# The feed-forward's linear half takes its 1/rms behind w_down, and six pairs of w_up instead of five go by seven products

## The chip, the core and the metric

One core of a Trainium2 chip runs the whole program in one launch. The metric is the device time of that launch in microseconds (us). TensorE (PE) does the matrix products; its weight loads are listed apart as PEld. VectorE (DVE) and ScalarE (ACT) do everything between the products, GpSimd (POOL) a little, and SyncE (SP) starts most of the DMA transfers. Sums of products are gathered in PSUM banks of 512 float32 columns; all other data on the core lies in SBUF.

## The reference

The program is a trunk of two layers over 528 tokens (16 learned meta tokens and 512 frames) with 1024 features. Each layer has a mixer, which the change doesn't touch, and a gated feed-forward with a causal convolution over three tokens:

```
n = rms_norm(h, norm_ffn[l])                    # n = h * 1/rms(h, per token) * gain per feature
gate, up = split(n @ w_up, 2)                   # w_up: 1024 x 5632, halves of 2816
gate = causal_dwconv(gate, conv_w)              # 3 taps over tokens, one weight per feature
h = h + (silu(gate) * up) @ w_down              # w_down: 2816 x 1024
```

1/rms is one number per token. The gate half must have it before the convolution and the silu. The linear half, `up`, is only multiplied by something and then summed over features, so a factor per token may stand before or behind w_down. The meta tokens are dropped from the output of the second layer.

## The kernel before, in words

Features lie on the 128 partitions, tokens on the free axis. Every float32 product is made of three passes of TensorE: operands are split into a high part and a rest (`wh` and `wl` of the weights, made by ScalarE at L242 and VectorE at L243; likewise for the activations, by `feed` at L187 and L188), and high x high, high x rest and rest x high are added up in one bank. Below, "product" is one such pass: one matmul instruction of 128 x 128 weights and 264 tokens (or 256, or 512, in the second layer).

w_up runs over 22 pairs j: the gate tile 2j and the linear tile 2j+1, 128 features each. A plain pair is two times 96 products (L268; in the second layer the linear tile takes 48 products of 512 tokens). For each j in the list `UP`, `up7` does both tiles together by Strassen's scheme with seven block products instead of eight, in Winograd's form: two feature tiles by two halves of the tokens, 84 products (L284), with sums of weight blocks (L302 to L305, VectorE) and of result banks (L1097 to L1107, VectorE). Gate banks come from the tags "g" and "a" in turn, the linear half of plain pairs from "s" and "a" in turn, two banks each; `up7` uses g or a, s, and x.

Behind the products of a pair, VectorE multiplies the gate by `rb`, which holds 1/rms of every token on all partitions (L1130, or L1133 while emptying the banks), the convolution and the tanh follow (L1138, L1140, L1141), VectorE multiplies the linear half by `rb` too (L1143 or L1148) and then by the gate `cv` (L1149). The result is split into high part and rest; for the last eight j it is also brought into the sums that the seven products of w_down want.

w_down takes the eight output tiles in four steps of two (m0 = 0, 2, 4, 6). In each step, `strassen` does features 14 to 21 by seven products (84 instructions, L284) and `others` does features 0 to 13 in chunks of four (168 products in layer 0, L1245; products of 512 tokens in most of layer 1). In the first step the seven products come last but one chunk, in the others first. Within the block of seven products, bank X1 is filled, copied by ScalarE into SBUF tile `ts` (L1219), and filled again; X2 is filled; from X1, X2 and the copy VectorE makes four sums in `ts` and `tu` (L1222 to L1227), of 128 x 264 each. They are added to the residual `hk` by `addto` (L1211) before the second chunk of `others` of the step (in the first step before its last chunk). At the end of the step the four banks C are added to `hk` by the same function (or two wide banks at L1263), and in layer 0 each finished `hk` is stored and fed to the next norm: ScalarE makes its high part and its square (L187, L194), VectorE the rest and the sum of squares (L188, L195).

Two things set the order around the change. First, each engine works through its instructions in the order that the compiler's priorities gave, and the splits of weights and the sums of weight blocks have a high priority, so they are put among older work. Second, tiles of one tag share a few buffers: `ts`, `tu`, the tanh `th` and the square `sqt` of `feed` share two (tag "th"); `hk` and `uu` share two; the staged weights have four (`wst`), their split parts three each. An allocation waits until the oldest user of its buffer is done.

Of the kernel before, what the change touches and what calls it, by code (L numbers as in the profile page):

```python
# [11 lines left out]
F32R = mybir.dt.float32r  # L12
# [16 lines left out]
INV = -2e38  # L29
UP = (2, 5, 8, 11, 14)  # L30

# [73 lines left out]
AR = 6720  # L105
# [9 lines left out]
def _trunk(es, tc, nc, a):  # L115
    pool = lambda n, b, **k: es.enter_context(tc.tile_pool(name=n, bufs=b, **k))
    p1 = pool("p1", 1)
# [5 lines left out]
    V, S, G, PE = nc.vector, nc.scalar, nc.gpsimd, nc.tensor  # L123
# [948 lines left out]
    def ffn(l, nf, h1, t0):  # L1072
# [40 lines left out]
        for j in range(FT):  # L1113
            if j == J0:
                far = p1.tile([128, AR], F32R, tag="ar", name="far")
            if j % 2 == 0:
# [10 lines left out]
            if j in UP:  # L1127
                uu = p2.tile([128, T], F32, tag="hk", name="uu", bufs=2)
                up7(j, cs, uu)
                V.tensor_tensor(cs[:, 2 + t0:2 + T], cs[:, 2 + t0:2 + T], rb[:, t0:], op=mul)  # L1130
            else:
                for p, t in ps:
                    V.tensor_tensor(cs[:, 2 + t.start:2 + t.stop], p, rb[:, t], op=mul)  # L1133
# [6 lines left out]
            S.activation(th[:, t0:], cv[:, t0:], AF.Tanh, scale=0.5)  # L1140
            V.scalar_tensor_tensor(cv[:, t0:], th[:, t0:], 1.0, cv[:, t0:], op0=add, op1=mul)  # L1141
            if j in UP:
                V.tensor_tensor(uu[:, t1:], uu[:, t1:], rb[:, t1:], op=mul)  # L1143
            else:
                ps = pu0 if j == 0 else dense(a["w_up"][l, 2 * j + 1], KT, lambda k, part: X[k][:, part], t1, "sa"[j % 2])
                uu = p2.tile([128, T], F32, tag="hk", name="uu", bufs=2)
                for p, t in ps:
                    V.tensor_tensor(uu[:, t], p, rb[:, t], op=mul)  # L1148
            V.tensor_tensor(uu[:, t1:], uu[:, t1:], cv[:, t1:], op=mul)  # L1149
            if j >= J0:  # L1150
# [36 lines left out]
        for m0 in range(0, 8, 2):  # L1187
# [20 lines left out]

            def addto(i, x):
                d = hks[i // 2][:, (s1, s2)[i % 2]]  # L1210
                V.scalar_tensor_tensor(d, x, 0.5, d, op0=mul, op1=add)  # L1211

            def strassen():
                tt = p2.tile([128, T], F32, tag="th", name="ts", bufs=2)
                tu = p2.tile([128, T], F32, tag="th", name="tu", bufs=2)
                P1, U2, U3, U4 = tt[:, :nh], tt[:, nh:2 * nh], tu[:, :nh], tu[:, nh:2 * nh]

# [15 lines left out]
                seven(src, range(J0, FT, 4), S7, sums, X1, X2, C[0], C[1], C[2], first, (one, mid, end))  # L1233
                return P1, U4, U3, U2

# [16 lines left out]
            for k0 in ks[:n]:  # L1252
                others(k0)
            us = strassen()
            for i, k0 in enumerate(ks[n:]):
                if i == 1 or m0 == 0:
                    for c, x in enumerate(us):
                        addto(c, x)
                others(k0)
            for u in range(2):  # L1260
                hk, m = hks[u], m0 + u
                if wide:
                    V.scalar_tensor_tensor(hk[:, t1:], cb[u][:, :2 * nh], 0.5, hk[:, t1:], op0=mul, op1=add)  # L1263
                else:
                    for h in range(2):
                        addto(2 * u + h, C[2 * u + h])
                if last:
                    for t in (s1, s2) if m == 7 else [slice(NM, T)]:
                        nc.sync.dma_start(a["out"][:, m, t.start - NM:t.stop - NM], hk[:, t])
                else:  # L1270
                    t = dr.tile([128, T], F32, name=f"g{l}_{m}")
                    nc.sync.dma_start(t, hk)
                    h2.append(t)
                    nn.feed(m, hk)
# [75 lines left out]
```

## Time and profile before

| | |
|---|---|
| time, median of 3 runs | 1697.04 us (1694.74 to 1697.94) |
| the profiled execution's own time | 1696.78 us |
| its span in the profile | 1695.0 us |
| mean granted clock of TensorE | 0.998 |
| TensorE busy | 1682.9 us, 99% of the span, 13476 instructions |
| VectorE busy | 1360.1 us, 80% |
| ScalarE busy | 819.0 us, 48% |
| GpSimd busy | 75.8 us, 4% |
| DMA | 173.81 MB, mean 103 GB/s |

An engine's busy time is the sum over its instructions, overlaps counted once. The span goes from the first instruction to the last; the execution's own time has what lies around it too. The granted clock is a share of full speed, 1.00 being the level of 2.4 GHz and 0.50 that of 1.2 GHz. In timelines, an instruction's duration goes from its issue to its end; instructions of one engine overlap, so what one costs in a dense stretch is the time from its issue to the next one's issue. An idle time with its releaser is printed in square brackets where the engine stood still.

### The profile page before, as it was taken

The page shows a single profiled execution, that of the slowest core. Times are in us where ns is not written, and L with a number is a line of the kernel's source. Part 1 is how long each engine was busy: PE and PEld are TensorE (multiplying, and loading weights), DVE is VectorE, ACT ScalarE, POOL GpSimd, SP SyncE. Part 2 cuts the span into 40 slices and gives each one's busy share as a digit, 9 for nine tenths or more (in the row PEclk, how much of TensorE's full clock was granted, in tenths as well). Part 3 has the DMA queues.
Part 4 walks back from the last instruction along what each step waited for, and adds up shares of the span by engine and source line. Part 5 has one row for each costly group of instructions (what it writes and reads, how often), then busy time and mean ns, then how long its engine had stood idle before and what let it go on. Part 6 is the DMA issues. An engine that isn't in the chain of part 4 may idle for free.

```text
span 1695.0 us, 35229 instructions
## 1 busy us (share of the span) xinstructions
PE 1682.9 (99%) x13476; PEld 1579.7 (93%) x13476; DVE 1360.1 (80%) x3229; ACT 819.0 (48%) x1779; POOL 75.8 (4%) x190
## 2 busy tenths in 40 slices
PE   9999999999999999999999999999999999999999
PEld 8899988889999999999998999888899999999888
DVE  7899899866788888766558998998767888887754
ACT  6553556553444444434335534566635544444432
POOL 1000111100000000000100000110000000000000
PEclk9999999999999999999999999999999999999999
DMA  6322211225533333234433222112255433333443
GB/s 209 98 64 88 76 46 51 73 75 174 174 121 95 99 94 94 88 104 145 156 103 99 63 88 82 52 45 76 70 176 174 125 94 94 95 98 94 127 123 100
DMA packets 95097, 173.81 MB, mean 103 GB/s; under 512 B 10704, under 2 KB 15536, under 8 KB 94672
## 3 DMA queue, kind: packets, MB, share of 16 engines
q1 hardware_dynamic: 93456, 167.01, 32.5%
q10 hardware_dynamic: 1472, 4.54, 0.7%
q8 instruction: 106, 1.74, 0.4%
q14 instruction: 63, 0.52, 0.1%
HBM read 154.04 MB, written 17.06 MB: 101 GB/s over the span
## 4 chain that ended last, share of the span: by engine, by line
PE 90%; DVE 6%; ACT 3%; issue 1%; DMA 0%; ACTq 0%; DVEq 0%
PE a L268 55%; PE a L284 10%; PE a L1245 9%; PE misc L347 2%; PE iq L347 2%; PE vps L784 2%; PE oBT L947 1%; PE isc L530 1%; PE tps L795 1%; DVE wl L243 1%; PE logit L923 1%; PE PTp L941 1%; PE dS L838 1%; ACT ar L833 0%; ACT wh L242 0%
## 5 line engine op out<-in xcount | busy, mean ns | idle before, releaser
L268 PE MATMUL a<-X,wh 128*128 128x264 f32 (+4 forms) x4208 | 837.1, 295 | 0.6 <-DVE cs L1133 0.6
L268 PEld LDWEIGHTS a<-X,wh 128*128 128x128 f32 x4208 | 666.9, 189 | 17.7 <-issue 1.4
L268 PE MATMUL a<-X,wl 128*128 128x264 f32 (+4 forms) x2104 | 618.4, 294 | 0.0
L242 ACT ACTIVATE wh<-wst 128x512 fp32r<-128x512 f32 (+2 forms) x512 | 309.5, 605 | 537.7 <-PE a L268 284.6
L243 DVE TENSOR_TENSOR wl<-wst,wh 128x512 fp32r<-128x512 f32 (+2 forms) x512 | 335.8, 656 | 153.3 <-ACT wh L242 138.3
L268 PEld LDWEIGHTS a<-X,wl 128*128 128x128 f32 x2104 | 397.9, 189 | 9.1
L1245 PE MATMUL a<-F,wh 128*128 128x264 f32 (+2 forms) x728 | 154.8, 309 | 0.0
L1245 PEld LDWEIGHTS a<-F,wh 128*128 128x128 f32 x728 | 118.0, 188 | 7.3
L1245 PE MATMUL a<-F,wl 128*128 128x264 f32 (+2 forms) x364 | 112.7, 310 | 0.0
L268 PE MATMUL a<-Y,wh 128*128 128x264 f32 (+2 forms) x512 | 92.9, 283 | 0.0
L268 PEld LDWEIGHTS a<-Y,wh 128*128 128x128 f32 x512 | 79.1, 188 | 0.0
L268 PE MATMUL a<-Y,wl 128*128 128x264 f32 (+2 forms) x256 | 72.5, 283 | 0.0
L1245 PEld LDWEIGHTS a<-F,wl 128*128 128x128 f32 x364 | 68.6, 188 | 3.8
L1138 DVE SCALAR_TENSOR_TENSOR cv<-cs,vec,cv 128x528 f32<-128x528 f32 (+1 forms) x88 | 66.7, 758 | 2.7 <-ACT cv L1136 2.1
L405 DVE SCALAR_TENSOR_TENSOR cv<-cs,vec,cv 128x528 f32<-128x528 f32 x72 | 54.4, 758 | 0.9 <-ACT cv L403 0.8
L888 DVE MAX8 m<-ar 128x8 f32<-128x256 f32 (+2 forms) x96 | 53.2, 554 | 1.1
L889 DVE MATCH_REPLACE8 ar<-m,ar 128x256 f32<-128x256 f32 (+2 forms) x96 | 51.9, 541 | 0.0
L268 PEld LDWEIGHTS a<-Y,wl 128*128 128x128 f32 x256 | 48.2, 188 | 0.0
L284 PE MATMUL a<-F,wh 128*128 128x264 f32 (+1 forms) x256 | 47.9, 284 | 0.0
L284 PE MATMUL a<-xar,wh 128*128 128x264 f32 (+1 forms) x240 | 45.6, 283 | 0.0
L1140 ACT ACTIVATE th<-cv 128x528 f32<-128x528 f32 (+1 forms) x44 | 28.1, 638 | 35.7 <-DVE cv L1138 35.6
L284 PE MATMUL a<-X,wh 128*128 128x264 f32 (+1 forms) x240 | 44.8, 283 | 0.0
(401 smaller groups left out, 3057.1 us busy)
## 6 DMA issues: line engine op xcount, KB each, us to landing
wst<-w_up SPq DMA_DIRECT2D x176, 256.0 KB, 2.7
wst<-w_down SPq DMA_DIRECT2D x80, 256.0 KB, 2.7
wst<-w_a SPq DMA_DIRECT2D x64, 256.0 KB, 2.7
wst<-w_gate SPq DMA_DIRECT2D x64, 256.0 KB, 2.9
wst<-w_out SPq DMA_DIRECT2D x32, 256.0 KB, 2.9
hk<-h SPq DMA_DIRECT2D x24, 264.0 KB, 3.5
tg<-gg SPq DMA_DIRECT2D x16, 264.0 KB, 2.2
gr<-tg SPq DMA_DIRECT2D x16, 264.0 KB, 2.7
```

Source lines behind the costliest of these rows:

```text
L242: S.activation(h, w, AF.Copy)
L243: V.tensor_tensor(lo, w, h.bitcast(F32), op=sub)
L268: mms.append(PE.matmul(ps[j][:, :t.stop - t.start], w[:, ws], x[:, t], start=(kk == 0 and w is h and part == 0), stop=(kk == kts - 1 and w ...
L284: PE.matmul(o, ww[:, c:c + 128], x[:, part], start=st, stop=False, skip_group_check=True)
L347: mms.append(PE.matmul(b[:, c:], X[kk][:, part, o:o + 128], w[:, c:], start=(kk == 0 and w is h and part == 0), stop=(kk == KT - 1 and w i ...
L405: V.scalar_tensor_tensor(cv, cs[:, i:i + T], vc(cw + i), cv, op0=mul, op1=add)
L784: PE.matmul(p[r, ch], Ml[r, ch], U[r, ch], start=True, stop=True)
L888: V.max(m8, sc)
L889: V.match_replace(sc, m8, sc, SEL)
L1138: V.scalar_tensor_tensor(cv[:, t0:], cs[:, t0 + i:i + T], vec[:, cw + i:cw + i + 1], cv[:, t0:], op0=mul, op1=add)
L1140: S.activation(th[:, t0:], cv[:, t0:], AF.Tanh, scale=0.5)
L1245: PE.matmul(o, ww[:, 128 * k:128 * k + 128], Yf[k0 + k][:, part, t], start=first(2 * u + h) if k == 0 and part == 0 and ww is w[0] else False,
```

## The change

Two edits. `UP`, the list of pairs of w_up done by seven products, goes from five pairs to six, at other places. And the linear half of the feed-forward is no longer multiplied by 1/rms ahead of the gate: banks (or `uu`) are multiplied by `cv` directly. The factor is applied behind w_down: the four sums in `ts` and `tu` stay there until the end of the step, the C banks are added to them, the sum is multiplied by `rb` in place, and half of that is added to the residual. `addto` goes. The sums are laid out so that `ts` holds both halves of the first output tile and `tu` those of the second. In the last step of the last layer (`tail`) the sums are scaled and added to `hk` before the second chunk, and each half's C bank at the end by itself.

```diff
@@ -27,7 +27,7 @@
 SEL = -3e38
 SP = 4
 INV = -2e38
-UP = (2, 5, 8, 11, 14)
+UP = (2, 4, 7, 9, 12, 14)
 
 
 V_CONVA, V_CONVF, V_BG, V_AON = 0, 48, 114, 130
@@ -1111,8 +1111,6 @@
                   X1, X2, b0, b1, b2, lambda i: True if i is not None else False, (one, mid, end))
 
         for j in range(FT):
-            if j == J0:
-                far = p1.tile([128, AR], F32R, tag="ar", name="far")
             if j % 2 == 0:
                 yt = p1.tile([128, 4 * T], F32R, tag=f"Q{j // 2}", name=f"F{j // 2}")
             y = yt.rearrange("p (a b t) -> p a b t", a=2, b=2)[:, j % 2]
@@ -1127,6 +1125,9 @@
             if j in UP:
                 uu = p2.tile([128, T], F32, tag="hk", name="uu", bufs=2)
                 up7(j, cs, uu)
+            if j == J0:
+                far = p1.tile([128, AR], F32R, tag="ar", name="far")
+            if j in UP:
                 V.tensor_tensor(cs[:, 2 + t0:2 + T], cs[:, 2 + t0:2 + T], rb[:, t0:], op=mul)
             else:
                 for p, t in ps:
@@ -1139,14 +1140,14 @@
             th = p2.tile([128, T], F32, tag="th", name="th", bufs=2)
             S.activation(th[:, t0:], cv[:, t0:], AF.Tanh, scale=0.5)
             V.scalar_tensor_tensor(cv[:, t0:], th[:, t0:], 1.0, cv[:, t0:], op0=add, op1=mul)
+
             if j in UP:
-                V.tensor_tensor(uu[:, t1:], uu[:, t1:], rb[:, t1:], op=mul)
+                V.tensor_tensor(uu[:, t1:], uu[:, t1:], cv[:, t1:], op=mul)
             else:
                 ps = pu0 if j == 0 else dense(a["w_up"][l, 2 * j + 1], KT, lambda k, part: X[k][:, part], t1, "sa"[j % 2])
                 uu = p2.tile([128, T], F32, tag="hk", name="uu", bufs=2)
                 for p, t in ps:
-                    V.tensor_tensor(uu[:, t], p, rb[:, t], op=mul)
-            V.tensor_tensor(uu[:, t1:], uu[:, t1:], cv[:, t1:], op=mul)
+                    V.tensor_tensor(uu[:, t], p, cv[:, t], op=mul)
             if j >= J0:
 
                 ys = yt[:, :8 * nh].rearrange("p (a b t) -> p a b t", a=4, b=2)
@@ -1206,14 +1207,10 @@
                 begun.add(b)
                 return r
 
-            def addto(i, x):
-                d = hks[i // 2][:, (s1, s2)[i % 2]]
-                V.scalar_tensor_tensor(d, x, 0.5, d, op0=mul, op1=add)
-
             def strassen():
                 tt = p2.tile([128, T], F32, tag="th", name="ts", bufs=2)
                 tu = p2.tile([128, T], F32, tag="th", name="tu", bufs=2)
-                P1, U2, U3, U4 = tt[:, :nh], tt[:, nh:2 * nh], tu[:, :nh], tu[:, nh:2 * nh]
+                P1, U4, U3, U2 = tt[:, :nh], tt[:, nh:2 * nh], tu[:, :nh], tu[:, nh:2 * nh]
 
                 def one():
                     S.activation(P1, X1, AF.Copy)
@@ -1231,7 +1228,7 @@
                             p2.tile([128, T], F32, tag="cv", name="s34", bufs=2)[:, :512])
 
                 seven(src, range(J0, FT, 4), S7, sums, X1, X2, C[0], C[1], C[2], first, (one, mid, end))
-                return P1, U4, U3, U2
+                return tt[:, :2 * nh], tu[:, :2 * nh]
 
             def others(k0):
                 kn = min(WC, J0 - k0)
@@ -1252,18 +1249,29 @@
             for k0 in ks[:n]:
                 others(k0)
             us = strassen()
+            tail = last and m0 == 6
             for i, k0 in enumerate(ks[n:]):
-                if i == 1 or m0 == 0:
-                    for c, x in enumerate(us):
-                        addto(c, x)
+                if tail and i == 1:
+                    for hk, w in zip(hks, us):
+                        V.tensor_tensor(w, w, rb[:, t1:], op=mul)
+                        V.scalar_tensor_tensor(hk[:, t1:], w, 0.5, hk[:, t1:], op0=mul, op1=add)
                 others(k0)
             for u in range(2):
-                hk, m = hks[u], m0 + u
-                if wide:
-                    V.scalar_tensor_tensor(hk[:, t1:], cb[u][:, :2 * nh], 0.5, hk[:, t1:], op0=mul, op1=add)
+                hk, m, w = hks[u], m0 + u, us[u]
+                if tail:
+                    for h, t in enumerate((s1, s2)):
+                        x = w[:, nh * h:nh * h + nh]
+                        V.tensor_tensor(x, C[2 * u + h], rb[:, t], op=mul)
+                        V.scalar_tensor_tensor(hk[:, t], x, 0.5, hk[:, t], op0=mul, op1=add)
                 else:
-                    for h in range(2):
-                        addto(2 * u + h, C[2 * u + h])
+                    if wide:
+                        V.tensor_tensor(w, w, cb[u][:, :2 * nh], op=add)
+                    else:
+                        for h in range(2):
+                            x = w[:, nh * h:nh * h + nh]
+                            V.tensor_tensor(x, x, C[2 * u + h], op=add)
+                    V.tensor_tensor(w, w, rb[:, t1:], op=mul)
+                    V.scalar_tensor_tensor(hk[:, t1:], w, 0.5, hk[:, t1:], op0=mul, op1=add)
                 if last:
                     for t in (s1, s2) if m == 7 else [slice(NM, T)]:
                         nc.sync.dma_start(a["out"][:, m, t.start - NM:t.stop - NM], hk[:, t])
```

The compiler's new order shows in three places. Names carry a running number; the same tile has a slightly different number in the two kernels.

On ScalarE, at the step from m0 = 2 to m0 = 4 of w_down in layer 0: `hk` is one of the two residual tiles of the step that ends, X2 and X3 the high parts of the next norm's input, `sqt` squares, `ts` <- `a` the copy of the new block's X1, `wh` high parts of weights (`s12`, `s34`: of sums of weight blocks). Before:

```order
L187 ACTIVATE X2_10512<-hk_10135,gains_79 128x528
L242 ACTIVATE wh_10603<-wst_10550 128x256
L194 ACTIVATE sqt_10515<-hk_10135 128x528
L187 ACTIVATE X3_10522<-hk_10137,gains_79 128x528
L242 ACTIVATE wh_10613<-s12_10556 128x512
L194 ACTIVATE sqt_10525<-hk_10137 128x528
L242 ACTIVATE wh_10629<-s12_10562 128x512
L242 ACTIVATE wh_10647<-s34_10557 128x512
L1219 ACTIVATE ts_10538<-a_10536 128x264
L242 ACTIVATE wh_10663<-s34_10563 128x512
```

After:

```order
L242 ACTIVATE wh_10602<-wst_10549 128x256
L242 ACTIVATE wh_10612<-s12_10555 128x512
L187 ACTIVATE X2_10509<-hk_10134,gains_79 128x528
L242 ACTIVATE wh_10628<-s12_10561 128x512
L242 ACTIVATE wh_10646<-s34_10556 128x512
L194 ACTIVATE sqt_10512<-hk_10134 128x528
L187 ACTIVATE X3_10521<-hk_10136,gains_79 128x528
L194 ACTIVATE sqt_10524<-hk_10136 128x528
L1216 ACTIVATE ts_10537<-a_10535 128x264
L242 ACTIVATE wh_10662<-s34_10562 128x512
```

The copy stood right behind the high parts of three sums, and both feeds (X2, X3) ahead of these or among them. Now the high parts stand around the first feed, and its square, the second feed, the second square and the copy follow one another.

On VectorE, layer 0, behind the seven products of pair 2 of w_up: `cs` is the gate, here of pair 3 from its two banks `a`, `uu` the linear half of pair 2, `cv` and `th` the convolved gate of pair 2 and its tanh, `wsum` sums of weight blocks for the next seven-product pair (5 before, 4 now). Before:

```order
L1106 TENSOR_TENSOR uu_6766<-a_6769,pu_6772 128x264
L1107 TENSOR_TENSOR uu_6766<-a_6770,pu_6772 128x264
L1138 SCALAR_TENSOR_TENSOR cv_6915<-cs_6764,vec0_158,cv_6915 128x528
L1143 TENSOR_TENSOR uu_6766<-uu_6766,rb_6595 128x528
L243 TENSOR_TENSOR wl_7034<-wst_7031,wh_7033 128x512
L1138 SCALAR_TENSOR_TENSOR cv_6915<-cs_6764,vec0_158,cv_6915 128x528
L1133 TENSOR_TENSOR cs_6988<-a_6926,rb_6595 128x264
L1141 SCALAR_TENSOR_TENSOR cv_6915<-th_6919,cv_6915 128x528
L1133 TENSOR_TENSOR cs_6988<-a_6927,rb_6595 128x264
L243 TENSOR_TENSOR wl_7073<-wst_7070,wh_7072 128x512
```

After:

```order
L1107 TENSOR_TENSOR uu_6764<-a_6768,pu_6770 128x264
L302 TENSOR_TENSOR wsum_7073<-wst_7076 128x256
L303 TENSOR_TENSOR wsum_7073<-wst_7074,wst_7076 128x256
L304 TENSOR_TENSOR wsum_7073<-wsum_7073,wst_7074 128x256
L1139 SCALAR_TENSOR_TENSOR cv_6913<-cs_6762,vec0_158,cv_6913 128x528
L243 TENSOR_TENSOR wl_7031<-wst_7028,wh_7030 128x512
L305 TENSOR_TENSOR wsum_7073<-wst_7074,wsum_7073 128x256
L1139 SCALAR_TENSOR_TENSOR cv_6913<-cs_6762,vec0_158,cv_6913 128x528
L1134 TENSOR_TENSOR cs_6985<-a_6923,rb_6595 128x264
L1134 TENSOR_TENSOR cs_6985<-a_6924,rb_6595 128x264
L243 TENSOR_TENSOR wl_7079<-wst_7074,wh_7078 128x512
```

The multiplication of `uu` by `rb` (L1143) is gone; four sums of weight blocks stand ahead of the two lines that empty pair 3's gate banks (L1133 before, L1134 now).

On VectorE, at the same step of w_down as the first pair of listings: `hk` of the step that ends, its C banks `a`, `wl` the rests of weights, `sqacc` the sum of squares. Before:

```order
L1211 SCALAR_TENSOR_TENSOR hk_10135<-a_10139,hk_10135 128x264
L243 TENSOR_TENSOR wl_10553<-wst_10548,wh_10552 128x512
L305 TENSOR_TENSOR s34_10563<-wst_10548,s12_10562 128x256
L1211 SCALAR_TENSOR_TENSOR hk_10135<-a_10140,hk_10135 128x264
L243 TENSOR_TENSOR wl_10594<-wst_10542,wh_10593 128x256
L1211 SCALAR_TENSOR_TENSOR hk_10137<-a_10141,hk_10137 128x264
L1211 SCALAR_TENSOR_TENSOR hk_10137<-a_10142,hk_10137 128x264
L188 SCALAR_TENSOR_TENSOR X2_10512<-hk_10135,gains_79,X2_10512 128x528
L243 TENSOR_TENSOR wl_10604<-wst_10550,wh_10603 128x256
L195 TENSOR_TENSOR sqacc_9743<-sqacc_9743,sqt_10515 128x528
L188 SCALAR_TENSOR_TENSOR X3_10522<-hk_10137,gains_79,X3_10522 128x528
L243 TENSOR_TENSOR wl_10614<-s12_10556,wh_10613 128x512
```

After:

```order
L1272 TENSOR_TENSOR tu_10145<-tu_10145,a_10140 128x264
L243 TENSOR_TENSOR wl_10603<-wst_10549,wh_10602 128x256
L1274 SCALAR_TENSOR_TENSOR hk_10134<-ts_10144,hk_10134 128x528
L1272 TENSOR_TENSOR tu_10145<-tu_10145,a_10141 128x264
L243 TENSOR_TENSOR wl_10613<-s12_10555,wh_10612 128x512
L1273 TENSOR_TENSOR tu_10145<-tu_10145,rb_6595 128x528
L243 TENSOR_TENSOR wl_10629<-s12_10561,wh_10628 128x512
L243 TENSOR_TENSOR wl_10647<-s34_10556,wh_10646 128x512
L188 SCALAR_TENSOR_TENSOR X2_10509<-hk_10134,gains_79,X2_10509 128x528
L195 TENSOR_TENSOR sqacc_9742<-sqacc_9742,sqt_10512 128x528
L1274 SCALAR_TENSOR_TENSOR hk_10136<-tu_10145,hk_10136 128x528
L188 SCALAR_TENSOR_TENSOR X3_10521<-hk_10136,gains_79,X3_10521 128x528
```

Before, each C bank went to the residual by itself and the feeds' rests (L188) followed at once, ahead of the rests of the sums of weight blocks. Now a C bank is added to `ts` or `tu` (L1272), the two are multiplied by `rb` (L1273) and added to the residuals (L1274); three rests of sums stand ahead of the first feed's rest.

On TensorE, 43 products of the block stood ahead of the second filling of X1 at this step, now 54 do: products for X2 and for the third C bank were put there.

## Rows read from the trace of the kernel before

**Rows 1.** The page's first part: busy us, share of the span, instructions.

```profile
PE 1682.9 (99%) x13476; PEld 1579.7 (93%) x13476; DVE 1360.1 (80%) x3229; ACT 819.0 (48%) x1779; POOL 75.8 (4%) x190
```

**Rows 2.** The chain of waits, stage of w_up: start us, us, engine, line, instructions.

```profile
573.17 10.24 PE a L284 x84
583.41 23.49 PE a L268 x192
...
1383.88 10.09 PE a L284 x84
1393.96 22.67 PE a L268 x144
```

**Rows 3.** The chain of waits, w_down of layer 0.

```profile
764.11 4.29 PE a L284 x35
...
775.24 14.51 PE a L1245 x119
...
806.60 14.51 PE a L1245 x119
...
837.98 20.48 PE a L1245 x168
```

**Rows 4.** Timeline of VectorE, w_down: start us, us, operation, shapes, [idle before <-releaser].

```profile
793.72 0.69 DVE L243 TENSOR_TENSOR wl<-wst,wh 128x512 fp32r<-128x512 f32 x1
794.32 0.42 DVE L303 TENSOR_TENSOR s<-wst 128x256 f32<-128x256 f32 x1
...
794.99 0.43 DVE L1211 SCALAR_TENSOR_TENSOR hk<-a,hk 128x264 f32<-128x264 f32 x1
...
798.64 0.70 DVE L195 TENSOR_TENSOR sqacc<-sqacc,sqt 128x528 f32<-128x528 f32 x1
799.26 0.76 DVE L188 SCALAR_TENSOR_TENSOR X<-hk,gains,X 128x528 fp32r<-128x528 f32 x1
799.94 1.91 DVE L243 TENSOR_TENSOR wl<-s,wh 128x512 fp32r<-128x512 f32 x3
```

**Rows 5.** Timeline of VectorE, layer 0, end of pair 2 of w_up.

```profile
516.35 0.70 DVE L1130 TENSOR_TENSOR cs<-cs,rb 128x528 f32<-128x528 f32 x1
```

**Rows 6.** Timeline of TensorE, first products of three blocks and one into X1.

```profile
515.78 0.41 PE L268 MATMUL a<-X,wh 128*128 128x264 f32 x2
...
795.55 0.41 PE L284 MATMUL a<-F,wh 128*128 128x264 f32 x2
...
801.38 0.49 PE L284 MATMUL a<-F,wh 128*128 128x264 f32 x2
...
1631.86 0.40 PE L284 MATMUL a<-F,wh 128*128 128x256 f32 x2
```

**Rows 7.** What TensorE waits for, w_up of layer 1: us, times, longest.

```profile
PE a L268 <- DVE cs L1133: 0.6, 3, 0.2
```

**Rows 8.** Timeline of ScalarE, w_down of layer 0, two steps.

```profile
769.72 0.72 ACT L187 ACTIVATE X<-hk,gains 128x528 fp32r<-128x528 f32 x1
770.35 0.63 ACT L194 ACTIVATE sqt<-hk 128x528 f32<-128x528 f32 x1
770.88 0.36 ACT L1219 ACTIVATE ts<-a 128x264 f32<-128x264 f32 x1
...
800.95 0.36 ACT L1219 ACTIVATE ts<-a 128x264 f32<-128x264 f32 x1
```

**Rows 9.** Timeline of VectorE, w_down of layer 1.

```profile
1632.28 0.42 DVE L243 TENSOR_TENSOR wl<-wst,wh 128x256 fp32r<-128x256 f32 x1
1632.62 1.28 DVE L1263 SCALAR_TENSOR_TENSOR hk<-a,hk 128x512 f32<-128x512 f32 x2
```

**Rows 10.** Timeline of VectorE, end of the kernel.

```profile
1690.89 0.42 DVE L1211 SCALAR_TENSOR_TENSOR hk<-a,hk 128x256 f32<-128x256 f32 x1 [0.27 <-PE a L1245]
1691.60 0.42 DVE L1211 SCALAR_TENSOR_TENSOR hk<-a,hk 128x256 f32<-128x256 f32 x1 [0.29 <-PE a L1245]
```

**Rows 11.** Stretch, us, busy us (instructions) by engine, PEclk, DMA share, GB/s.

```profile
1032.60:1036.00 3.40, 3.40 (x19) 3.40 (x17) 2.34 (x15) 1.74 (x11) 0.03 (x1) 0.50 0.26 80
```

## The prediction

> **What bounds the kernel now.** I read four views in this order. First the page's busy line: TensorE is busy for 1682.9 of 1695.0 us and no other engine comes near it [rows 1]. Then the chain of waits in order of time, which says what TensorE does in that time: one product of 264 tokens after another, evenly spaced. Two pairs of w_up done as plain products take 23.49 us in the first layer and 22.67 us in the second; a pair done by seven products takes 10.24 us for 84 of them (0.122 us each) and 10.09 us [rows 2]. So a product less is time less, and a wait of TensorE is time more, nothing else counts. Third, the places where TensorE does wait: in the w_down stage of layer 0 the step from one pair of output tiles to the next. From 764.11 to 775.24 us a block of seven products takes 11.13 us instead of 10.24; the next two periods of 31.4 us (775.24, 806.60, 837.98) hold 168 + 84 = 252 products, worth 30.7 us [rows 3]. That makes delays of 0.9, 0.65 and 0.65 us. Last, the timelines of VectorE and ScalarE around the middle one, which show why: from 793.72 us on VectorE runs without a gap [rows 4]. That place, and not the removed multiplications, decides this change.
>
> **The change part by part.**
>
> *A sixth pair by seven products, in each layer.* Layer 0: 23.49 / 2 = 11.75 us become 10.24: -1.50 us. Layer 1: 22.67 / 2 = 11.34 become 10.09: -1.25 us. Together -2.75 us [rows 2], all of it on TensorE's path.
>
> *The multiplication by 1/rms of the linear half goes.* Per pair VectorE loses one pass over 528 tokens (0.62 us from one issue to the next [rows 4]) 44 times, some 27 us, and gains the weight sums of the two extra seven-product pairs. VectorE is at 80% [rows 1] and TensorE doesn't wait for the passes removed: I count nothing. The evictions of the linear half now wait for the gate's convolution and tanh, but the banks that they hold are wanted again a pair later or 24 products into the next block, and by my walk along VectorE's order they are free by then: nothing, bounded by 0.3 us at each of the two places (6 to 7 and 8 to 9) in layer 0.
>
> *Seven-product pairs closer together.* After pairs 2 and 12 only one plain pair follows, so the weight sums of the next seven-product pair now stand in VectorE's order ahead of the eviction of the plain pair's gate (second order fence). From 516.35 us [rows 5] VectorE issues two 0.61 us passes, two of 0.34, three sums of 0.34, a convolution pass of 0.68, a split of 0.60, a sum of 0.34 and a convolution pass of 0.68: 5.2 us, so the eviction starts at 521.6 and ends at 522.0. The linear half wants that bank after 48 products of 0.122 us from 515.8 us [rows 6], at 521.6: a wait of 0.5 us, twice, +1.0 us. In layer 1 the wait of this kind is there now, three times, 0.6 us in all [rows 7]; two of the three places stay, somewhat longer: 0. Bounds of this part: 0 (VectorE comes in time) and +3 us (0.5 at every one of the six).
>
> *w_down, layer 0: what the whole sum turns on.* Until now half of the seven products' results were added to the residual early, and their two SBUF tiles (ts, tu) were free long before the next block. Now ts and tu live until the last chunk of w_down is done, are added to the other sums, multiplied by 1/rms and only then added to the residual. The next block needs a tile of this pair for its first step: ScalarE copies the bank X1 into the new ts, and until it has, TensorE may not start the second product into X1. In ScalarE's new order that copy stands behind the feeds of both residual tiles (first order fence), and the second feed waits for VectorE's last addition. The walk at the middle step, with today's issue gaps [rows 4, 9]: VectorE reaches its first addition at 794.99 us. Ten instructions follow: additions, sum and small splits 7 x 0.34, one split 0.60, one multiplication 0.62, one residual addition 0.68: 4.28 us, 799.27. Then the split of the first sum 0.60 (it waits 0.06 for ScalarE), the multiplication of tu 0.62, two splits 1.20, the feed's split 0.68, the squares 0.62: 803.05. The second residual addition takes 0.76 to its end: 803.81. ScalarE then feeds, squares and copies: 0.63 + 0.53 + 0.36 = 1.52 [rows 8], with 0.06 us of signal 805.4; TensorE took 0.07 us more after such a copy (today's copy of this step ended at 801.31 [rows 8], 0.07 us ahead of the X1 product at 801.38 [rows 6]). TensorE's new order has 54 products ahead of that one: 795.55 [rows 6] + 54 x 0.122 = 802.1. The delay is 3.3 us where it is 0.65 now. The same walk at the first step ends within 0.1 us of that, and the third has the same order. 3 x 3.3 = 9.9, less 0.9 + 0.65 + 0.65: +7.7 us. Bounds: a third of that (2.6), if VectorE and ScalarE overlap better than the walk has it, and +10, if the last split is late too (it has 0.1 us to spare). I take 7.7, since each gap in it is a row.
>
> The page "Perfetto Trace Analysis" of the Trainium skill (Optimizing Tensor Performance, Matmuls) says that groups of products should go round through different banks, so that emptying one lies beside the next group. X1 is filled twice within one block here; by that rule the copy decides, and this trace agrees: X1's second filling came 0.07 us after the copy's end [rows 6, 8].
>
> *w_down, layer 1.* No feeds follow, so the copy waits for the first residual addition alone, which is done in time. But VectorE has two additions, two multiplications and one residual addition ahead of the first sum's split: from 1632.28 us 0.34 + 0.60 + 0.60 + 0.34 + 3 x 0.60 = 3.7 us [rows 9] and 0.69 for the split, done at 1636.65; TensorE wants it after 38 products of 0.120 us from 1631.86 [rows 6], at 1636.4. Some 0.3 us at two steps and 0.4 at the first: +1.0 us, between 0 and 2.
>
> *The end.* Each of the last four halves gets a multiplication (0.42 us) ahead of its addition. One half comes from TensorE every 0.71 us [rows 10] and now costs VectorE 0.42 + 0.34 and a wait on itself, so it ends up three times 0.05 to 0.1 us behind: +0.7 us, between 0.42 and 1.0.
>
> *TensorE's clock.* At today's steps TensorE is held up by 0.9 us at most [rows 3]; the change makes three gaps of 2.5 to 3.3 us. The granted clock was 0.50 for 3.4 us at 1032.60 us [rows 11], in a stretch of few and small products. The same at one of the new gaps would cost at most half of 3.4 us, 1.7. Bounds 0 and 3 x 1.7 = 5.1 us; no row lies near, so I take the middle, 2.5 us.
>
> Sum: -2.75 + 1.0 + 7.7 + 1.0 + 0.7 + 2.5 = +10.2 us. The profiled execution took 1696.78 us (1.78 around its span), the median of three runs 0.26 us more. 1697.04 + 10.2 = 1707.
>
> **Rivals.**
> 1. *The copy of X1 isn't held up* (the additions come early enough, or TensorE has work to put ahead). For it: VectorE has 20% idle on average [rows 1]. Against it: none of that idle time lies at the step [rows 4], and all three engines run in order. It gives -2.75 + 1.0 + 1.0 + 0.7 - 2.2 (today's delays gone) = -2.3: 1695 us. This is the side of no change or slightly faster; it decides if the second residual addition ends before 800.5 us, 3.3 us earlier than the walk says. Chance 0.09.
> 2. *Half of it is hidden*: each step costs 1.7 us and the clock stays. -2.75 + 1.0 + (5.1 - 2.2) + 1.0 + 0.7 = +2.9: 1700 us. Chance 0.1.
> 3. *The clock falls after every gap.* 5.1 instead of 2.5: 1710 us. For it: the gaps are longer than any that TensorE has now. Against it: the products before and after are dense. Chance 0.2. The page "TensorE: Matmul & The Clock Gate" of the Trainium skill (Why this matters for your kernels) warns of gaps of such a size: they put TensorE back to its lower rate. No run here shows such a gap yet.
> 4. *VectorE becomes the bound of w_up* where seven-product pairs lie close: 0.6 us more at each of twelve such pairs, 7 us: 1714 us. Against it: it loses as much work there as it gets. Chance 0.05.
>
> **How the numbers follow.** The forecast has 0.56, with 1703 to 1709 as its own range. What three runs of this kernel can tell from no change is about 0.2%, 3.4 us: 1693.6 to 1700.4. Faster: a part of the first rival, 0.04. Within 0.2%: the rest of it and half of the second, 0.1. Slower: 0.86. The range reaches down to just above the second rival and up past the third: 1701 to 1712.
>
> **What would show it.** Right: in layer 0 each of the three later blocks of w_down takes 13 to 14 us for its 84 products, with one gap of 2.5 to 3.4 us ahead of the second product into X1, ended by ScalarE's copy of X1, which follows the second square at once; w_up shorter by 1.5 and 1.25 us less the waits at pairs 3 and 13; maybe a spell at clock 0.50 behind a gap. Wrong: blocks of 10.3 to 11 us there, or the copy early; then the time is below 1698. A time above 1712 would mean waits in w_up that I have not seen.

## The result and the profile after

The changed kernel takes 1709.33 us (median of 6 runs, 1706.68 to 1711.38) against 1697.18 us; the ratio is 1.0073, 95% interval 1.006 to 1.0086. It is 12.2 us slower. 1707 was forecast, with a range of 1701 to 1712; the narrower 1703 to 1709, given as the forecast's own, was missed by 0.3 us. The profiled execution took 1706.68 us, the fastest of the six, with a span of 1704.9 us: 9.9 us above the span of before.

The page's first line after (columns as in [rows 1]):

```profile
PE 1682.3 (99%) x13476; PEld 1577.5 (93%) x13476; DVE 1356.7 (80%) x3224; ACT 820.1 (48%) x1789; POOL 75.0 (4%) x190
```

TensorE's busy time is the same to 0.6 us, and the span grew by 9.9: what was added is nearly all waiting, and this line can't say where. (The count of 13476 is the same too, though the kernel has another pair by seven products in each layer. A plain pair is 96 products in layer 0 and 72 in layer 1, since a row of [rows 2] holds two pairs, and not twice as many; with 84 in their place, one layer loses 12 and the other gains 12.) What TensorE waits for, over the whole span, in the kernel after (us in total, times, longest):

```profile
PE a L284 <- ACT ts L1216: 7.6, 3, 2.7
PE a L268 <- DVE cs L1134: 2.0, 3, 0.9
...
PE a L268 <- ACT wh L242: 0.7, 1, 0.7
```

The first row is new: three waits for ScalarE's copy of X1. The second is the wait of [rows 7], for the gate's emptied bank: 0.86 and 0.77 us at pairs 3 and 13 of layer 0, 0.35 at pair 13 of layer 1. The third row is pair 3 of layer 1. The profile puts it down to the high part of a weight, which ended last, at 1376.19 us; the gate's bank was empty only 0.05 us before that. Where the time lies by stage, from TensorE's timeline (w_up from the sums of its norm to the first product of w_down, w_down to the end of its last product):

| us | before | after | the difference |
|---|---|---|---|
| w_up, layer 0 | 247.46 | 249.02 | +1.56 |
| w_down, layer 0 | 125.51 | 134.71 | +9.20 |
| w_up, layer 1 | 240.98 | 240.09 | -0.89 |
| w_down, layer 1 | 119.22 | 120.09 | +0.87 |
| behind the last product | 3.44 | 4.31 | +0.87 |
| all else (not changed) | 958.39 | 956.68 | -1.71 |

Without the last row the change costs 11.6 us, near the 12.2 of the medians. That row is the spread of two executions: in the mixer the one of before had two spells of 3.4 us at a granted clock of 0.50, from 182.7 us and from 1032.6 us [rows 11], and the one of after had none there.

The step from m0 = 2 to m0 = 4 in layer 0, the chain of waits after (start us, us, what), where before [rows 3] had 31.4 us from one block of seven products to the next and TensorE's timeline now has 34.0 (800.49 to 834.49):

```profile
800.65 2.84 PE a L284 x23
...
804.78 0.58 DVE tu L1273
805.36 0.04 issue
805.40 1.29 DVE wl L243 x2
806.69 0.68 DVE X L188
807.37 0.62 DVE sqacc L195
807.99 0.63 DVE hk L1274
808.62 0.02 issue
808.64 0.73 ACT X L187
809.38 0.53 ACT sqt L194
809.91 0.28 ACT ts L1216
810.19 0.04 issue
810.24 3.93 PE a L284 x30
```

The chain is to be read backwards from 810.24: product into X1, the copy, a square, the second feed, and from there VectorE without a gap. ScalarE was idle ahead of that feed, in its timeline after:

```profile
808.64 0.73 ACT L187 ACTIVATE X<-hk,gains 128x528 fp32r<-128x528 f32 x1 [2.29 <-DVE hk L1274]
809.28 0.63 ACT L194 ACTIVATE sqt<-hk 128x528 f32<-128x528 f32 x1
809.82 0.37 ACT L1216 ACTIVATE ts<-a 128x264 f32<-128x264 f32 x1
```

The copy costs 0.37 us, as in [rows 8]. What it waits in is ScalarE's queue, 2.29 us of it with nothing to do, and two operations of 0.64 and 0.54.

### The profile page after: what moved, and what is told of

The parts are those of the page before. It is cut to its first block, busy times and chain, and to the rows that moved or that the text cites. A ratio compares the mean times of both kernels' runs of the same rounds, so it can differ in the third digit from the quotient of the medians.

```text
span 1704.9 us, 35266 instructions
## 1 busy us (share of the span) xinstructions
PE 1682.3 (99%) x13476; PEld 1577.5 (93%) x13476; DVE 1356.7 (80%) x3224; ACT 820.1 (48%) x1789; POOL 75.0 (4%) x190
## 4 chain that ended last, share of the span: by engine, by line
PE 88%; DVE 7%; ACT 3%; issue 1%; DMA 1%; ACTq 0%; DVEq 0%
PE a L268 53%; PE a L284 10%; PE a L1242 9%; PE misc L347 2%; PE iq L347 2%; PE vps L784 2%; PE oBT L947 1%; DVE wl L243 1%; PE isc L530 1%; PE tps L795 1%; PE logit L923 1%; PE PTp L941 1%; ACT wh L242 1%; DMA wst<-w_up 1%; PE dS L838 0%
## 5 line engine op out<-in xcount | busy, mean ns | idle before, releaser
L268 PE MATMUL a<-X,wh 128*128 128x264 f32 (+3 forms) x4096 | 812.0, 294 | 2.7 <-DVE cs L1134 2.0
L268 PEld LDWEIGHTS a<-X,wh 128*128 128x128 f32 x4096 | 646.7, 188 | 18.9 <-ACT wh L242 2.9
L268 PE MATMUL a<-X,wl 128*128 128x264 f32 (+4 forms) x2048 | 600.4, 293 | 0.0
L268 PEld LDWEIGHTS a<-X,wl 128*128 128x128 f32 x2048 | 386.1, 189 | 8.7
L1242 PEld LDWEIGHTS a<-F,wh 128*128 128x128 f32 x728 | 118.0, 188 | 7.3
L284 PE MATMUL a<-F,wh 128*128 128x264 f32 (+1 forms) x256 | 50.1, 290 | 7.6 <-ACT ts L1216 7.6
L284 PE MATMUL a<-xar,wh 128*128 128x264 f32 (+1 forms) x288 | 54.8, 284 | 0.3 <-DVE uu L1150 0.3
L284 PE MATMUL a<-X,wh 128*128 128x264 f32 (+1 forms) x288 | 53.8, 283 | 0.0
L284 PEld LDWEIGHTS a<-F,wh 128*128 128x128 f32 x256 | 40.9, 193 | 9.1 <-ACT ts L1216 8.6
```

The costliest lines, as they stand in the source:

```text
L268: mms.append(PE.matmul(ps[j][:, :t.stop - t.start], w[:, ws], x[:, t], start=(kk == 0 and w is h and part == 0), stop=(kk == kts - 1 and w ...
L284: PE.matmul(o, ww[:, c:c + 128], x[:, part], start=st, stop=False, skip_group_check=True)
L1242: PE.matmul(o, ww[:, 128 * k:128 * k + 128], Yf[k0 + k][:, part, t], start=first(2 * u + h) if k == 0 and part == 0 and ww is w[0] else False,
```

## The experiments

**The two parts, each alone.**

In the kernel before, the new list alone:

```diff
-UP = (2, 5, 8, 11, 14)
+UP = (2, 4, 7, 9, 12, 14)
```

> The kernel before with only the list of pairs changed to (2, 4, 7, 9, 12, 14); the linear half keeps its multiplication by 1/rms ahead of the gate. My theory (the loss lies in w_down of layer 0, where ScalarE's copy of X1 waits behind the feeds): two pairs save 2.75 us, waits of TensorE for VectorE at pairs 3 and 13 and at a block of seven products give back 2 to 4 us: 1696 to 1699 us, w_down as before, no gap ahead of the second filling of X1. Rival A (the places of the pairs carry the loss, by the sums of weight blocks ahead of the evictions): 1705 to 1709 us.

Measured: 1698.06 against 1695.73 us, ratio 1.0008 (0.9999 to 1.0018). w_down of layer 0 takes 125.62 us, as before. Rival A falls. But w_up gained nothing from one plain pair less in each layer: 248.30 and 241.37 us against 247.46 and 240.98. The time is as expected and the places too (pairs 3 and 13), but TensorE's largest wait in w_up is not one for VectorE:

```profile
PE a L284 <- ACT wh L242: 2.6, 4, 0.7
```

In this kernel the compiler put four products of the next block by seven (L284) ahead of the linear half of the plain pair, and four times the first of them waits 0.65 us for the high part of a weight.

In the changed kernel, the old list:

```diff
-UP = (2, 4, 7, 9, 12, 14)
+UP = (2, 5, 8, 11, 14)
```

> The changed kernel with the old list (2, 5, 8, 11, 14): only the place of 1/rms is changed. My theory: w_down of layer 0 loses the same 9.2 us as in the changed kernel (blocks of 13.7 to 15.1 us instead of 10.7 to 11.3), layer 1's w_down and the end 0.9 us each, w_up stays as before: 1707 to 1709 us. Rival A: 1697 to 1700 us.

Measured: 1706.62 us, ratio 1.006 (1.0045 to 1.0075), 10.9 us above. w_down of layer 0 takes 133.12 us, each of its three later blocks 13.68 from the first product's start to the last one's end, and TensorE's longest wait is the same:

```profile
PE a L284 <- ACT ts L1216: 7.6, 3, 2.7
```

The loss belongs to the place of 1/rms, whichever pairs are done by seven products. One thing was not expected: w_up of layer 1 took 239.63 us, 1.35 less than before. The passes removed had been worth something there, and I had counted nothing. In the kernel before, VectorE's timeline at pair 3 of layer 1 has the pass over the linear half of pair 2 two places ahead of the eviction that TensorE waits for:

```profile
1364.98 0.69 DVE L1143 TENSOR_TENSOR uu<-uu,rb 128x512 f32<-128x512 f32 x1
...
1366.18 0.42 DVE L1133 TENSOR_TENSOR cs<-a,rb 128x256 f32<-128x256 f32 x1
```

Without that pass the three waits of [rows 7] are gone. They had been printed as 0.2 us each, but each stretch of plain pairs behind them takes 0.45 us less (two pairs 22.84 instead of 23.28).

**The copy's place in ScalarE's queue.** An own tile makes the compiler put the copy ahead of both feeds (shown for layer 0; layer 1 reads the first quarter from that tile too):

```diff
-                P1, U4, U3, U2 = tt[:, :nh], tt[:, nh:2 * nh], tu[:, :nh], tu[:, nh:2 * nh]
+                pc = p1.tile([128, 1024], F32, tag="ikT", name="pc")
+                P1, U4, U3, U2 = pc[:, :nh], tt[:, nh:2 * nh], tu[:, :nh], tu[:, nh:2 * nh]
...
-                            V.tensor_tensor(x, x, C[2 * u + h], op=add)
+                            V.tensor_tensor(x, x if u or h else P1, C[2 * u + h], op=add)
```

> The changed kernel, but ScalarE copies X1 into a tile of its own (the one that up7 uses, free in w_down), which is free again after the first addition of a C bank; the copy then stands ahead of both feeds in ScalarE's order. The result of the first quarter is added from that tile. My theory: the gap of 2.2 to 2.7 us ahead of X1's second filling goes at each of the three steps, the blocks take 10.4 to 11.5 us, the time falls by 6 to 8 us to 1700 to 1703 us, and TensorE's clock is 0.998 in all runs. Rival B (VectorE's longer chain bounds the step itself, the copy is only the last of it): TensorE waits for splits of the weight sums instead, 1 to 2 us per step, 1704 to 1707 us. Rival C (much of the loss is the lower clock of some executions, which has other causes): the clock stays between 0.995 and 0.998.

Measured: 1696.99 us against 1695.73, ratio 1.0008 (0.9999 to 1.0018). The chain of waits at the same step of that run:

```profile
796.27 7.32 PE a L284 x60
803.59 0.62 DVE sqacc L195
804.21 0.62 DVE hk L1284
804.83 0.61 DVE wl L243
805.44 0.04 issue
805.48 0.76 PE a L1243 x4
806.25 1.45 PE a L284 x12
```

VectorE still works through the same additions (sqacc, residual, a split), but what TensorE wants from it now is a split that ends just in time: the chain passes to TensorE 0.04 us behind it, and TensorE's timeline shows no gap of 0.15 us or more in the whole stage. ScalarE's timeline of that run has the copy ahead of both feeds, 6.34 us ahead of the second one, which still ends late:

```profile
798.52 0.39 ACT L1217 ACTIVATE pc<-a 128x264 f32<-128x264 f32 x1 [0.44 <-DVE tu L1282]
...
804.86 0.74 ACT L187 ACTIVATE X<-hk,gains 128x528 fp32r<-128x528 f32 x1 [0.73 <-DVE hk L1284]
```

w_down of layer 0 takes 124.25 us, 1.3 us less than before the change. Rival B falls: VectorE's longer chain harms only through the copy. About 11 of the 12.2 us came back, more than the 6 to 8 expected: w_down is shorter than before, so part of the delays of [rows 3] went too, and what the clock had cost (below). One thing more changed in this run, and it was not tried by itself: the compiler put seven products of the next chunk ahead of the block's last twelve, so up to 0.9 us per step may be TensorE's new order and not the copy. The Trainium skill's page "Perfetto Trace Analysis" (Optimizing Tensor Performance, Matmuls) wants groups of products to go round through different banks; here the bank stayed the same, and with the copy 6 us earlier no gap was left.

**The price of the chain.** The two multiplications by 1/rms of each step are left out in layer 0:

```diff
-                    V.tensor_tensor(w, w, rb[:, t1:], op=mul)
+                    if l:
+                        V.tensor_tensor(w, w, rb[:, t1:], op=mul)
```

> The changed kernel without the two multiplications by 1/rms per step of w_down in layer 0, so its linear half lacks that factor in layer 0; everything else stands. It prices the chain ahead of the copy. My theory: both multiplications (0.62 us each from issue to issue) stand ahead of the second residual addition, so each of the three gaps shrinks by about 1.2 us, 3.7 us in all: about 1705.5 us. If the copy is held by something else on ScalarE (its high parts of the weight sums), the gaps stay at 2.2 to 2.7 us and the time at 1708 to 1710.

Measured: 1701.32 us, ratio 1.0029 (1.0019 to 1.0039). That is 5.6 us above the kernel before beside it, where the changed kernel was 12.2 above: 6.6 us came back. What TensorE waits for in w_down of layer 0 in that run:

```profile
PE a L284 <- ACT ts L1216: 2.7, 3, 1.2
```

The gaps were 2.2, 2.7 and 2.7 us and are 0.3, 1.2 and 1.2: 1.5 less at the later two, where I had priced 1.24. The direction and the place are as expected, the size is larger. The compiler also put the first feed of each step further ahead among ScalarE's high parts of weight sums; that this makes the difference is not shown. By the stages w_down of layer 0 takes 128.00 us, 6.7 less than in the profile of the changed kernel, 1.4 of that the spell told of next.

**The clock.** The changed kernel again, beside the kernel before, for the clock of each execution.

> The changed kernel once more, beside the kernel before on the same chip, for the granted clock of each execution. My theory: a gap of 2 to 3 us in TensorE can be followed by a spell at clock 0.50 that costs 1.4 us, in some executions after none of the three gaps and in some after several; so the mean clock of its executions is lower than that of before (0.996 to 0.999 against 0.999 to 1.0) and its time is 11 to 13 us above before where the trace's gaps give 10. Rival C: the clock is spread as before's is, and the difference is 10 us.

Measured: 1708.9 us against 1696.11, ratio 1.0072 (1.006 to 1.0084). Spans and mean clocks of its six executions: 1703.3 us at 0.999, 1704.4 at 1.0, 1707.0 at 0.997, 1707.1 at 0.997, 1708.2 at 0.996, 1711.0 at 0.995. The 29 executions of the kernel before on that chip lie between 1693.2 and 1696.5 us, at 0.998 to 1.0, and the ten of the run with the copy's own tile between 1694.3 and 1697.2, at the same clocks. Rival C falls: the difference is 12.8 us, and the clock is spread more widely than before's. A mean of 0.998 is no sign of the gaps, since the kernel before has it by its two spells in the mixer. But lower means come with the gaps alone: 10 of the 16 executions with all three long gaps (the changed kernel twice, and it with the old list) lie at 0.995 to 0.997, and none of the 84 of the other experiments and of the 74 of the kernel before beside them. One spell is to be seen in the first profile of the changed kernel: two windows of 2.8 us that start behind the first and the second gap (columns: busy us and instructions of PE, PEld, DVE, ACT, POOL, then PEclk, DMA share, GB/s):

```profile
774.85:777.65 2.80, 2.80 (x12) 2.80 (x13) 1.56 (x3) 0.63 (x1) 0.00 (x0) 0.50 0.37 109
810.24:813.04 2.80, 2.80 (x23) 2.80 (x24) 2.21 (x5) 1.69 (x3) 0.00 (x0) 1.00 0.39 109
```

At the level of 0.50 (1.2 GHz) TensorE does 12 products where it does 23 at 2.4 GHz, and both rows say "busy". The 30 products behind the first gap took 5.33 us, those behind the second 3.93: 1.4 us. The profile of the second run of the changed kernel has no spell at its gaps, though these are as long (2.17, 2.72 and 2.71 us), nor has the run with the old list at its three: nine gaps in three profiles, one spell. The Trainium skill's page "TensorE: Matmul & The Clock Gate" (Why this matters for your kernels) warns that long idle gaps between bursts of products put TensorE back to its lower rate. This trace agrees for one gap of three, and that one was the shortest; before's two spells in the mixer came behind no gap at all (no wait of 0.15 us or more from 170 to 182.7 us and from 1000 to 1032.6 us). Why a spell comes in one execution and not in another no run here explains.

**w_up: why a sixth pair gains nothing.** VectorE's timeline after, behind the seven products of pair 2 in layer 0:

```profile
517.18 0.42 DVE L1107 TENSOR_TENSOR uu<-a,pu 128x264 f32<-128x264 f32 x1
518.06 0.43 DVE L302 TENSOR_TENSOR wsum<-wst 128x256 f32<-128x256 f32 x1 [0.46 <-DMA wst<-w_up]
...
521.37 0.76 DVE L1134 TENSOR_TENSOR cs<-a,rb 128x264 f32<-128x264 f32 x2
```

The sums of weight blocks (L302) wait 0.46 us for their weights to land, and the eviction (L1134) stands behind them in the queue. TensorE's timeline there:

```profile
521.94 0.48 PE L268 MATMUL a<-X,wh 128*128 128x264 f32 x2 [0.86 <-DVE cs L1134]
```

The gate and the linear half of pair 3 use the same two banks (tag a), hence the wait. With other banks, in the kernel before with the new list:

```diff
-                ps = pu0 if j == 0 else dense(a["w_up"][l, 2 * j + 1], KT, lambda k, part: X[k][:, part], t1, "sa"[j % 2])
+                ps = pu0 if j == 0 else dense(a["w_up"][l, 2 * j + 1], KT, lambda k, part: X[k][:, part], t1, "s" if j - 1 in UP else "sa"[j % 2])
```

> The kernel before with the new list of six pairs (the multiplication by 1/rms stays ahead of the gate), and the linear half of a plain pair that follows a pair by seven products takes its banks from tag s instead of a. My theory of the waits in w_up: in pairs 3 and 13 gate and linear half use the same two banks, so that the linear half waits for VectorE to empty the gate, which stands behind the sums of weight blocks; with other banks the wait goes and the 2.75 us of two pairs show: 1.5 to 2.7 us faster than before. Rival: VectorE and the weight buffers are simply late where seven-product pairs lie close; then the waits move elsewhere and it stays at 1 to 2 us slower than before, as with the pairs alone.

Measured: 1693.91 us against 1696.11, ratio 0.9986 (0.9977 to 0.9995): faster than both kernels. w_up takes 246.96 and 238.38 us. The waits for high parts of the run with the pairs alone are gone as well; the compiler put the linear half straight behind the gate again. The chain of waits of w_up, layer 1, has no wait left:

```profile
1348.86 10.09 PE a L284 x84
1358.94 11.34 PE a L268 x72
1370.28 10.09 PE a L284 x84
1380.37 22.67 PE a L268 x144
```

In layer 0 only 0.5 of the 1.5 us shows. Three blocks by seven products that follow a single plain pair take 10.70 to 10.79 us there instead of 10.41, by delays too short for the list of waits; the chain passes through VectorE and the weights' DMA ahead of two of them. The copy's own tile and these banks together, on the changed kernel:

> The changed kernel with ScalarE's copy of X1 in its own tile, and the same banks from tag s. My theory: the waits of 0.8 and 0.4 us for the emptied gate go, but the linear half now leaves its banks only behind the gate's tanh, and the next pair wants bank s 24 products after its start, so up to 0.9 us comes back there: between 0 and 1 us faster than with the own tile alone, that is 0 to 1.3 us slower than before. Rival: all of the waits go, 1 us faster than before.

Measured: 1694.67 us, ratio 0.9991 (0.9982 to 0.9999), 1.4 us faster than before: the rival's side. w_up is 1.3 us shorter in each layer than with the own tile alone. Some waits came back, as expected, 0.9 us in three in layer 0:

```profile
PE a L284 <- DVE uu L1150: 0.9, 3, 0.4
```

And seven pairs, on the kernel before:

> As the one with six pairs and s banks on the kernel before, but seven pairs (2, 4, 6, 8, 10, 12, 14). A seventh pair is worth 1.50 + 1.25 us more. If VectorE has room: 4 to 5.5 us faster than before. If weight staging and VectorE are late in every second pair, 0.4 to 0.6 us come back at each of twelve places: 0 to 2 us slower than before. I expect 2 to 4 us faster.

Measured: 1695.75 us, ratio 0.9995 (0.9987 to 1.0004): a miss, no gain that can be measured. w_up takes 247.73 and 238.48 us, no less than with six pairs, though a seventh is worth 2.75 us. Among VectorE's waits in layer 0 the staged weights have grown, five waits for DMA, 2.8 us, where the run with six pairs had three, 1.0 us:

```profile
DVE wsum L302 <- DMA wst<-w_up: 2.8, 5, 1.4
```

Whether they alone eat the gain was not tried.

**Two more versions.** In layer 1 the old place of 1/rms, in layer 0 the new one with the copy's own tile; and the old place with the own tile; both with six pairs and s banks.

> Six pairs with s banks; the linear half's 1/rms behind w_down in layer 0 only, with ScalarE's copy in its own tile; layer 1 keeps the multiplication ahead of the gate and the early additions. My theory: layer 0 as in the run with own tile and s banks (w_up 247.4, w_down 124.7 us), layer 1's w_down and the end give back 0.5 to 0.9 us each: about 1 us faster than that run, 2 to 3 us faster than the kernel before. Rival: layer 1's waits come from the pairs' places and not from the late 1/rms: no faster than that run.

Measured: 1693.46 us against 1696.46, ratio 0.9983 (0.9974 to 0.9992), 3.0 us faster than before. Against the run with the own tile and s banks the end gave 0.7 us, w_up and w_down of layer 1 0.5 and 0.3 by their profiles; by the times the two can't be told apart (0.9974 to 0.9992 and 0.9982 to 0.9999).

> Six pairs with s banks on the kernel before (1/rms ahead of the gate), and ScalarE's copy of X1 in its own tile. In the kernel before the steps of w_down lose 0.9 + 0.65 + 0.65 us by VectorE's splits of the weight sums, not by the copy; my theory: the copy doesn't matter there, 0 to 0.5 us faster than the run with six pairs and s banks. Rival: the copy holds TensorE there too, 1 to 2 us faster.

Measured: 1693.94 us, ratio 0.9984 (0.9975 to 0.9993), and w_down of layer 0 takes 125.16 us where the run without the own tile took 125.55. As expected: with 1/rms ahead of the gate the copy holds nobody up. The four versions with six pairs and s banks can't be told from each other by their times; all are faster than both kernels.

## Why the prediction was right, step by step

- *The sum and its place: right.* 12.2 us slower where 10.2 was forecast, most of it in w_down of layer 0, by the wait that was named. Of the 2.0 us that the sum fell short, the term of the pairs below alone is more.
- *w_down, layer 0, +7.7: right, to 0.2 us.* The stage grew by 9.2 us, of which 1.4 is the clock's spell; 7.6 us with the old list of pairs, 7.5 in the second run of the changed kernel (132.97 us). Each step is 3.3 us late, as forecast. Its gap is 2.73 us at two steps; at the first it is 2.18, under the 2.5 forecast, behind two waits for splits of 0.19 and 0.16. The walk along VectorE's queue held by the step: it had the second residual addition start 8.06 us behind the first addition of a C bank (803.05 from 794.99), and it started 8.08 us behind it (807.91 from 799.83 in VectorE's timeline).
- *TensorE's clock, +2.5: the price right, the number luck.* A spell was priced at 1.7 us at most and cost 1.4. How many come was not known, and the middle of the bounds was taken. The profile shows one. Over the six executions of the second run the median span stands 3.75 us above the shortest; that of the kernel before's 29 stands 1.0 us above theirs. The difference is 2.75, but that all of it is the clock is not shown.
- *w_down of layer 1, +1.0, and the end, +0.7: right* (0.87 each). One row of the end, after, where [rows 10] had an addition alone; the halves keep VectorE busy one behind the other:

```profile
1700.89 0.42 DVE L1264 TENSOR_TENSOR tu<-a,rb 128x256 f32<-128x256 f32 x1
1701.34 0.42 DVE L1265 SCALAR_TENSOR_TENSOR hk<-tu,hk 128x256 f32<-128x256 f32 x1
```

- *Pairs closer together, +1.0: the place right, the size wrong.* w_up should have lost 2.75 us and grew by 0.67, so this term is 3.4 us, above its bound of 3: 3.1 in layer 0 (it should have lost 1.50 and grew by 1.56), 0.4 in layer 1. In layer 0 my walk had the sums find their weights in SBUF, where they waited 0.46 us for a DMA; TensorE needs more than the wait itself to be in step again (1.14 us from product to product at 521.94 for a wait of 0.86); and from pair 6 to 7, where I had counted nothing, it waits 0.34 us for VectorE's multiplication of the linear half.
- *The passes removed: counted at nothing, and wrong in layer 1.* TensorE did wait for them there: without them the three waits of [rows 7] go, 1.35 us (with the old list; 0.2 in layer 0, which no wait explains). In the changed kernel the new place of the pairs took this back and more: 238.38 us were to be had in layer 1 with the same pairs, and it took 240.09, 1.7 us more, at pairs 3 and 13 above all. So the 0.4 of layer 1 is two errors that nearly cancel.
- *One reading of before: not borne out.* The prediction saw X1's second filling start 0.07 us behind the copy and took the copy to be what decides there. But that product follows the one ahead of it by 0.11 us, as others do (801.38 and 801.27), and the wait of that step lies earlier, 0.33 us for a split of VectorE's:

```profile
800.68 0.39 PE L284 MATMUL a<-far,wl 128*128 128x264 f32 x1 [0.33 <-DVE wl L243]
```

  With six pairs and s banks an own tile for the copy brings w_down from 125.55 to 125.16 us only. The copy costs TensorE its 3.3 us per step once it stands behind the feeds.
- *The rivals.* That the copy is not held up would have needed an own tile. Half of it is not hidden: 3.3 us per step, not 1.7. The clock does not fall after every gap. That VectorE becomes the bound of w_up was half true, with 3.4 us instead of 7.

## What to carry to other kernels

Where an engine works in order, an operation of 0.37 us can cost 3 us by what stands ahead of it in its queue; so when a change makes a buffer live longer, look for the next user of that buffer, and for what its queue then puts ahead of it. Giving that one user a buffer of its own took a few lines here and brought back nearly the whole loss. And a product saved was worth nothing here while the group behind it waited for the same banks. A wait that is printed as 0.2 us can cost more than twice that.

## What was not expected of the hardware

TensorE's half clock behind a gap of 2.18 us in one execution, and not behind gaps of 2.73 us in the same one; the same half clock in the mixer of before, behind no gap; mean clocks of 0.995 to 1.0 for the same kernel on the same chip, and spans 7.7 us apart with them.
